# Second layer's output projection: three pairs of token tiles by seven block products instead of eight, with the sums that this takes on VectorE

## The chip, the cores and the metric

The kernel runs on one NeuronCore of one Trainium2 chip. The metric is the device time of one execution in microseconds (us): 958.06 us is the median of three runs of the kernel before (957.97, 958.06 and 960.04 us).

## The reference

Two layers of a decoder trunk work on 1,024 tokens of width 1,024. In each layer an input projection feeds three groups of heads (windowed attention, retention, gated linear attention); their outputs are gated, joined to a mix of width 1,024 and projected back:

```
y = jnp.concatenate([a_out, r_out, g_out], axis=-1) @ w_out
return x + gate * rms_norm(y, post_gain)
```

The change concerns this product `mix @ w_out` of the second layer, which is the last large work of the program. Everything is f32 in and out.

## The kernel before

**Two halves for one number.** TensorE works on f32r operands. To keep f32 accuracy each operand is held as a high part (`hi`, the value rounded to f32r) and a low part (`lo`, the rest), and a product takes three passes: hi by hi, lo by hi, hi by lo (`PASSES`). Each operand therefore costs one rounding copy (ScalarE or VectorE) and one subtraction (VectorE or GpSimd) before TensorE can use it.

**The output projection** (`y_half`, L1278 to L1286) takes one tile of 128 tokens and one half of 512 output columns at a time: 8 steps over the width by 3 passes are 24 matmuls of 128x512 into one of three PSUM banks called `mm`. The token tile is the stationary operand, the weights are the moving one; the two 256-column units of a half are read as one operand of two segments (`both`). There are 8 token tiles by 2 halves. ScalarE squares the result for the norm (L1285, with a sum over the row), VectorE multiplies it by the gain (L1286). The last half of the last tile is split into two of 256 columns (`y_last`, L1288 to L1305), so that the sums of the norm are nearly done when the last matmul ends.

**The finish** of a tile (`finish`, L1325 to L1334) loads the tile's residual from `xs` in HBM (SyncE's queue), forms `yg * r + x` on VectorE (L1330), and stores it from ScalarE's queue (`sx`), which stands in order with ScalarE's arithmetic: a store that waits for VectorE holds what ScalarE has to do behind it.

**The mix** reaches the projection through HBM. `head_norm_gate` (L1007) and `gate` (L1508) round the gated head outputs, subtract, and store both halves to `mixS`; `load_mix` (L1307) reads 1 MB per tile. The `gate` results of tokens 512 to 1,023 come late: while the projection of the first tiles runs, TensorE still has some attention products to make between its matmuls.

**What sets the order.** TensorE's instructions keep the order in which the code emits them (with generators, `job` and `pump`, that let other work in between products at due times from the table `L`). On the other engines a scheduler orders the instructions; each engine and each queue then works strictly in that order.

**Memory.** The weights and the transposed tokens share two arenas of places 0 to 6 (`PLACES`, `TOK`); small work buffers come from pools: `t2` (14 of 128x512), `st` (5), `smx` (6), `mx` (2 of 1 MB).

## Time and profile before

| | us |
|---|---|
| median of three runs | 958.06 |
| the profiled execution | 954.65 |
| its span, first to last instruction | 952.9 |
| TensorE busy in the span | 932.7 |
| VectorE busy | 637.4 |
| ScalarE busy | 474.1 |
| GpSimd busy | 222.6 |

The profiled execution was one of the shorter ones: it lies 3.4 us under the median of the runs. A profile row gives start, duration, engine, line, operation, tiles out and in, and in brackets how long the engine had been idle and what ended that. `PE` is TensorE, `DVE` VectorE, `ACT` ScalarE, `POOL` GpSimd, `SPq` and `ACTq` the queues that issue transfers.

### The profile page before, as it was taken

The page shows a single profiled execution, that of the slowest core. Times are in us where ns is not written, and L with a number is a line of the kernel's source. Part 1 is how long each engine was busy: PE and PEld are TensorE (multiplying, and loading weights), DVE is VectorE, ACT ScalarE, POOL GpSimd, SP SyncE. Part 2 cuts the span into 40 slices and gives each one's busy share as a digit, 9 for nine tenths or more (in the row PEclk, how much of TensorE's full clock was granted, in tenths as well). Part 3 has the DMA queues.
Part 4 walks back from the last instruction along what each step waited for, and adds up shares of the span by engine and source line. Part 5 has one row for each costly group of instructions (what it writes and reads, how often), then busy time and mean ns, then how long its engine had stood idle before and what let it go on. Part 6 is the DMA issues. An engine that isn't in the chain of part 4 may idle for free.

```text
span 952.9 us, 15951 instructions
## 1 busy us (share of the span) xinstructions
PE 932.7 (98%) x5645; PEld 770.1 (81%) x5645; DVE 637.4 (67%) x1372; ACT 474.1 (50%) x1157; POOL 222.6 (23%) x288
## 2 busy tenths in 40 slices
...
GB/s 320 323 135 122 161 84 122 196 49 115 107 200 80 100 133 189 226 253 256 171 169 175 92 187 32 101 187 67 56 101 111 94 82 81 166 177 177 308 200 66
DMA packets 124651, 142.26 MB, mean 149 GB/s; under 512 B 11566, under 2 KB 95384, under 8 KB 124572
## 3 DMA queue, kind: packets, MB, share of 16 engines
...
## 4 chain that ended last, share of the span: by engine, by line
PE 85%; DVE 3%; issue 2%; ACT 2%; POOL 0%; DMA 0%; DVEq 0%; SPq 0%; POOLq 0%; ACTq 0%
PE mm L171 67%; PE aux L171 14%; PE aux L186 4%; ACT smx L971 0%; DMA t<-tabS 0%; ACT L1026 0%; DVE t L856 0%; ACT L1025 0%; DVE t L1029 0%; DVE t L1027 0%; DVE t L157 0%; ACT mx L1160 0%; DVE smx L966 0%; DVE arena L508 0%; DVE arena L149 0%
## 5 line engine op out<-in xcount | busy, mean ns | idle before, releaser
L171 PE MATMUL mm<-arena,arena 128*128 128x512 f32 (+2 forms) x1512 | 309.6, 358 | 0.0
L171 PE MATMUL mm<-arena 128*128 128x512 f32 (+2 forms) x1392 | 285.8, 359 | 0.0
L171 PEld LDWEIGHTS mm<-arena,arena 128*128 128x128 f32 x1512 | 246.5, 189 | 40.1 <-issue 2.1
L171 PEld LDWEIGHTS mm<-arena 128*128 128x128 f32 x1392 | 228.9, 190 | 37.2 <-issue 1.2
L171 PE MATMUL mm<-arena,mx 128*128 128x512 f32 (+1 forms) x696 | 157.3, 384 | 0.0
L171 PEld LDWEIGHTS mm<-arena,mx 128*128 128x128 f32 x696 | 126.5, 188 | 26.1 <-issue 1.5
L508 POOL TENSOR_TENSOR arena<-st,arena 128x512 fp32r<-128x512 f32 x57 | 85.9, 1512 | 158.0 <-ACT arena L147 100.3
L147 ACT ACTIVATE t<-aux 128x512 f32<-128x512 f32 x64 | 37.1, 591 | 82.6 <-PE aux L186 39.6
L508 DVE TENSOR_TENSOR arena<-st,arena 128x512 fp32r<-128x512 f32 x63 | 63.0, 1014 | 6.9 <-ACT arena L147 3.5
L147 ACT ACTIVATE arena<-st 128x512 fp32r<-128x512 f32 x82 | 48.4, 623 | 31.1 <-PE mm L171 15.0
L1285 ACT ACTIVATE t<-mm 128x512 f32<-128x512 f32 x30 | 17.9, 598 | 91.0 <-PE mm L171 46.3
L971 ACT ACTIVATE smx<-smx,sm 128x129 f32<-128x129 f32 x128 | 50.1, 394 | 18.1 <-DVE sm L968 17.9
L975 POOL TENSOR_TENSOR smx<-smx,sm 128x512 f32<-128x512 f32 x32 | 35.2, 1099 | 82.5 <-DVE sm L974 78.7
L384 DVE SCALAR_TENSOR_TENSOR acc<-st,c_act,acc 128x512 f32<-128x512 f32 x60 | 45.6, 760 | 13.1 <-DMA st<-in_w_mod_dram 12.1
L562 POOL TENSOR_TENSOR sm<-sm,few 128x1 f32<-128x1 f32 x26 | 14.8, 570 | 150.3 <-DVE sm L561 147.6
L1286 DVE TENSOR_TENSOR t<-mm,modg 128x512 f32<-128x512 f32 x30 | 20.7, 689 | 42.4 <-ACT t L1285 42.4
L1330 DVE SCALAR_TENSOR_TENSOR t<-t,sm,t 128x512 f32<-128x512 f32 x32 | 25.5, 827 | 30.8 <-DMA t<-xs 15.7
L186 PE MATMUL aux<-c_ident,t 128*128 128x128 f32 x224 | 33.7, 274 | 4.1 <-DVE t L634 2.3
L186 PEld LDWEIGHTS aux<-c_ident,t 128*128 128x128 f32 x224 | 26.6, 140 | 10.5 <-DVE t L634 2.7
L966 DVE COPY_PREDICATED smx<-c_curmask,aux 128x256 f32<-128x256 int32 x64 | 25.5, 447 | 12.8 <-ACT smx L147 11.4
L370 POOL MEMSET acc<- 128x512 f32 x4 | 2.1, 529 | 130.2 <-PE aux L171 119.1
L851 DVE TENSOR_TENSOR t<-mm,sincos 128x128 f32<-128x128 f32 (+2 forms) x36 | 16.2, 450 | 23.7 <-ACT t L147 12.5
...
## 6 DMA issues: line engine op xcount, KB each, us to landing
...
```

The source lines that it names most:

```text
L147: A.activation(dst, src, AF.Copy)
L171: T.matmul(dst, lhsT, rhs, start=start, stop=stop)
L186: T.transpose(dst, src, idn)
L384: V.scalar_tensor_tensor(acc, wt, c_act[:, k:k + 1], acc, ALU.mult, ALU.add)
L508: i = (G if first == 0 and kc in LOG else V if first == 0 else eng(f"wlo{kc}")).tensor_tensor(wt[:, 1, 2 * kc:2 * kc + 2, 0:256], st, f(hi ...
L851: V.tensor_tensor(a4, s4, cs.unsqueeze(1).unsqueeze(1).to_broadcast((P, nh, 2, 32)), ALU.mult)
L966: V.copy_predicated(sv, curmask.unsqueeze(1).to_broadcast((P, 2, P)), pv[:, :, n // P - 1, :])
L971: A.activation(sm[:, h, :], sm[:, h, :], AF.Exp, bias=mx[:, h:h + 1], accum_out=sums[:, h:h + 1])
L975: eng("pn").tensor_tensor(sm[:, :, 0:128], sm[:, :, 0:128], rs.unsqueeze(2).to_broadcast((P, 4, P)), ALU.mult)
L1285: A.activation(yg, pm, AF.Square, accum_out=ss[:, nh:nh + 1])
L1286: V.tensor_tensor(yg, pm, modg[l][:, 512 * nh:512 * nh + 512], ALU.mult)
L1330: V.scalar_tensor_tensor(xt[j], yg[j], r, xt[j], ALU.mult, ALU.add)
```

## The change

In the second layer, token tiles 0 and 1 are still projected with 24 matmuls per half (`y_std`), halves 1 of both tiles first. Tiles 2 to 7 go in three pairs (`y_pair`). For a pair the tokens (2 tiles), the width (2 halves of 512) and the columns (2 halves of 512) make a 2x2 by 2x2 block product. Instead of eight block products (12 matmuls each: 4 steps by 3 passes) it makes seven, with sums of the operands and of the results (Winograd's form of Strassen's scheme).

- Four sums of weight blocks are made once, in four chunks of 128 rows (`combine`): the four blocks of a chunk are fetched from HBM again as f32, VectorE makes four differences, ScalarE and VectorE make `hi` and `lo` of the results. They go into places 0, 1, 2 and, after tiles 0 and 1 have used it for their half 1, place 4 (`combine_last`).
- Four sums of token blocks are made for each pair (`operands`): seven `hi`/`lo` pairs in all. For this the mix of tiles 2 to 7 is stored and loaded as plain f32 (`mixF`), and `gate` and `head_norm_gate` no longer split it.
- The results: `c11` is the sum of two products, `c21`, `c22` and `c12` take running sums. Bank `a` accumulates products 1, 6, 5 and 3 on top of each other, and ScalarE copies it out after products 1, 6 and 5 (L1423, L1431, L1438); the next product may add to the bank only when that copy is done. Bank `c` holds product 7 (copied out, L1434) and then product 4 on top.
- `y_last` is gone, in the first layer too; for tile 7 one half of the residual sum moves to ScalarE (scaling) and GpSimd (sum), and its store to SyncE's queue (`late`).

The engine of every sum is set in the table `EN` (`ct0` to `ct3`, `co1` to `co7`, `cs1` to `cs4`, `cg`, `cg2`: all VectorE). The diff, cut to its core:

```diff
+    mixF = dr.tile([NT, P, KT, P], F32, name="mixF")
...
-        copy("mh", sh, g1)
-        V.tensor_tensor(sl, g1, f(sh), ALU.subtract)
-        for a, (k, m) in enumerate((("smh", sh), ("sml", sl))):
-            dma(k, mixS[2 * p:2 * p + 2, :, a, kt0:kt0 + 2, :].rearrange("t p k q -> p t k q"),
-                f(m).rearrange("p (t k q) -> p t k q", t=2, k=2))
+        if l == DEPTH - 1 and p:
+            dma("smh", mixF[2 * p:2 * p + 2, :, kt0:kt0 + 2, :].rearrange("t p k q -> p t k q"),
+                g1.rearrange("p (t k q) -> p t k q", t=2, k=2))
+        else:
+            copy("mh", sh, g1)
+            V.tensor_tensor(sl, g1, f(sh), ALU.subtract)
+            for a, (k, m) in enumerate((("smh", sh), ("sml", sl))):
+                dma(k, mixS[2 * p:2 * p + 2, :, a, kt0:kt0 + 2, :].rearrange("t p k q -> p t k q"),
+                    f(m).rearrange("p (t k q) -> p t k q", t=2, k=2))
...
-    def y_last(l, mixt, ss, yg):
...
+    def load_block(l, kh, nh):
+        b = blk(BLK[kh][nh])
+        for i in range(4):
+            st = stage()
+            dma("lw", st, w_rows(l, 4 * kh + i, nh))
+            hi, lo = b[:, 0, i, :], b[:, 1, i, :]
...
+                copy(f"whi{i}", hi, st)
+                eng(f"wlo{i}").tensor_tensor(lo, st, f(hi), ALU.subtract)
+
+    def wide():
+        return gp.tile([P, 4, 129], F32, tag="smx", name=nm("wide"), bufs=SMB).rearrange("p h n -> p (h n)")[:, 0:512]
+
+    def fetch_chunk(l, i):
+        tl = []
+        for kh, nh in ((0, 0), (0, 1), (1, 1), (1, 0)):
+            t_ = wide() if i % 2 else stage()
+            dma("lw", t_, w_rows(l, 4 * kh + i, nh))
+            tl.append(t_)
+        return tl
...
+    def put(k, hi, lo, src):
+        A.activation(hi, src, AF.Copy)
+        eng(k).tensor_tensor(lo, src, f(hi), ALU.subtract)
+
...
+        V.tensor_tensor(b11, b12, b11, ALU.subtract)
+        less(b12, b22, b12)
+        less(b22, b22, b11)
+        less(b21, b21, b22)
+        for n, t_ in ((1, b22), (0, b11), (2, b12)):
+            put(f"ct{n}", blk(n)[:, 0, i, :], blk(n)[:, 1, i, :], t_)
+        return b21
+
+    def combine_last(i, t_):
+        b = blk(BLK[0][1])
+        put("ct3", b[:, 0, i, :], b[:, 1, i, :], t_)
...
+            for kh in range(2):
+                a = t2() if p == 1 or len(res) == 1 else stage()
+                dma("lmix", a.rearrange("p (k q) -> p k q", k=4), mixF[t, :, 4 * kh:4 * kh + 4, :])
+                res.append(a)
+        return res
...
+    def operands(raw):
+        a11, a12, a21, a22 = raw
...
+        for n, src, tag in (("1", a11, "kT0"), ("2", a12, "kT1")):
+            o = gp.tile([P, 1024], F32R, tag=tag, name=nm("op"), bufs=1)
+            keep(n, o[:, 0:512], o[:, 512:1024], src)
+        s1, s2 = wide(), wide()
+        eng("cs1").tensor_tensor(s1, a21, a22, ALU.add)
+        eng("cs2").tensor_tensor(s2, s1, a11, ALU.subtract)
+        eng("cs3").tensor_tensor(a21, a11, a21, ALU.subtract)
+        yield res
+        x = mix_tile().rearrange("p a k q -> p (a k q)")
+        keep("6", x[:, 0:512], x[:, 512:1024], s2)
+        keep("7", x[:, 1024:1536], x[:, 1536:2048], a21)
+        eng("cs4").tensor_tensor(a12, a12, s2, ALU.subtract)
+        x = mix_tile().rearrange("p a k q -> p (a k q)")
+        keep("5", x[:, 0:512], x[:, 512:1024], s1)
+        keep("4", x[:, 1024:1536], x[:, 1536:2048], a22)
+        hi, lo = [gp.tile([P, 512], F32R, tag="st", name=nm("op"), bufs=BST) for _ in range(2)]
+        keep("3", hi, lo, a12)
+        yield res
+
+    def product(dst, a, b, start):
...
+        for x, y in PASSES:
+            for k in range(4):
+                mult(dst, a[x][:, k, :], b[:, y, k, :], start and q == 0, q == 11, None, not start)
...
+    def y_pair(l, p, o, soon):
+        t0, t1_ = 2 * p, 2 * p + 1
+        last = p == NP_ - 1
+        a, b, c = mm(), mm(), mm()
+        g0, g1 = modg[l][:, 0:512], modg[l][:, 512:1024]
+        sA, sB = small(2), small(2)
+        product(a, o["1"], blk(BLK[0][0]), True)
+        c11 = wide()
+        A.activation(c11, a, AF.Copy)
+        product(b, o["2"], blk(BLK[1][0]), True)
+        V.tensor_tensor(c11, b, c11, ALU.add)
+        A.activation(b, c11, AF.Square, accum_out=sA[:, 0:1])
+        eng("cg").tensor_tensor(c11, c11, g0, ALU.mult)
+        soon(0)
+        product(a, o["6"], blk(1), False)
+        c21 = wide()
+        A.activation(c21, a, AF.Copy)
+        product(c, o["7"], blk(2), True)
+        m7 = t2()
+        A.activation(m7, c, AF.Copy)
+        soon(1)
+        product(a, o["5"], blk(0), False)
+        c22 = t2()
+        i0 = A.activation(c22, a, AF.Copy)
+        i1 = V.tensor_tensor(c22, c22, m7, ALU.add)
+        A.activation(m7, c22, AF.Square, accum_out=sB[:, 1:2])
+        eng("cg2").tensor_tensor(c22, c22, g1, ALU.mult)
+        with tc.issue_after(i0.ins), tc.issue_after(i1.ins):
+            soon(2)
+        product(c, o["4"], blk(BLK[0][1]), False)
+        V.tensor_tensor(c21, c, c21, ALU.add)
+        A.activation(c, c21, AF.Square, accum_out=sB[:, 0:1])
+        V.tensor_tensor(c21, c21, g0, ALU.mult)
+        job(finish(l, t1_, sB, [c21, c22], None, (0,) if last else ()))
+        pump()
+        soon(3)
+        c12 = t2()
+        b22 = blk(BLK[1][1])
+        if not last:
+            product(a, o["3"], b22, False)
+            A.activation(c12, a, AF.Square, accum_out=sA[:, 1:2])
+            V.tensor_tensor(c12, a, g1, ALU.mult)
+            job(finish(l, t0, sA, [c11, c12]))
+            pump()
+            return
...
+        V.tensor_scalar(r, sA[:, 0:1], 1.0 / D, EPS, ALU.mult, ALU.add)
+        product(a, o["3"], b22, False)
+        sq = A.activation(c12, a, AF.Square, accum_out=sA[:, 1:2])
+        q = V.scalar_tensor_tensor(r, sA[:, 1:2], 1.0 / D, r, ALU.mult, ALU.add)
+        root = G.tensor_tensor(r, r, mhalf[:, 0:1], ALU.pow)
+        with tc.issue_after(sq.ins), tc.issue_after(root.ins):
+            for x, y, r7, t, sl in late:
+                A.activation(y, y, AF.Copy, scale=r7)
+                G.tensor_tensor(x, y, x, ALU.add)
+        for x, y, r7, t, sl in late:
+            dma("lx", out[0, t * P:(t + 1) * P, sl], x)
         with tc.issue_after(q.ins):
-            V.tensor_tensor(yg[:, c], pm, modg[l][:, 768:1024], ALU.mult)
-        return r
+            V.tensor_tensor(c12, a, g1, ALU.mult)
+        job(finish(l, t0, sA, [c11, c12], r))
+        pump()
+
+    def last_output(l):
+        mx = [load_mix(l, t) for t in range(2)]
...
+        chunk = {0: fetch_chunk(l, 0), 1: fetch_chunk(l, 1)}
+        raw = load_pair(l, 1)
...
+        for n, (nh, t) in enumerate(((1, 0), (1, 1), (0, 0), (0, 1))):
+            y_std(l, t, nh, mx[t], ss[t], yg[t][nh])
+            held[n] = combine(l, n, chunk.pop(n))
+            if n < 2:
+                chunk[n + 2] = fetch_chunk(l, n + 2)
+            if n == 1:
+                for i in range(2):
+                    combine_last(i, held.pop(i))
+            if nh == 0:
+                job(finish(l, t, ss[t], yg[t]))
+                pump()
+            if n == 2:
+                prep = operands(raw)
+                o = next(prep)
+        for i in (2, 3):
+            combine_last(i, held.pop(i))
+        next(prep)
...
+        for p in range(1, NP_):
+            def soon(i, p=p):
+                if p + 1 < NP_:
+                    if i == 0:
+                        nxt["raw"] = load_pair(l, p + 1)
+                    elif i == 2:
+                        nxt["prep"] = operands(nxt["raw"])
+                        nxt["o"] = next(nxt["prep"])
+            y_pair(l, p, o, soon)
+            if p + 1 < NP_:
+                next(nxt["prep"])
+                o = nxt["o"]
...
+    late = []
...
+            if j in side:
+                late.append((xt[j], yg[j], r, t, sl))
+                continue
+            else:
+                V.scalar_tensor_tensor(xt[j], yg[j], r, xt[j], ALU.mult, ALU.add)
...
+            whole = (4, 2 if hf == 0 else 0)[l == DEPTH - 1]
+            if whole < 4:
+                dma("sm0", mixF[4 * hf + whole:4 * hf + 4, :, k, :].rearrange("t p q -> p t q"),
+                    ao[:, whole * P:].rearrange("p (t q) -> p t q", q=P))
+            if whole:
+                w_ = slice(0, whole * P)
+                mh, ml = t2(F32R), t2(F32R)
+                copy("mg", mh[:, w_], ao[:, w_])
+                eng("mgl").tensor_tensor(ml[:, w_], ao[:, w_], f(mh[:, w_]), ALU.subtract)
+                for a, m in ((0, mh), (1, ml)):
+                    dma(f"sm{a}", mixS[4 * hf:4 * hf + whole, :, a, k, :].rearrange("t p q -> p t q"),
+                        f(m[:, w_]).rearrange("p (t q) -> p t q", q=P))
...
+        if l == DEPTH - 1:
+            last_output(l)
+            return
...
-MIXP = (6, 7)
+BLK = ((3, 4), (5, 6))
```

TensorE, the last half of tile 1 and the products of tiles 2 and 3, before (each `mm` is a fresh use of one of the three PSUM banks, `mx` the tokens' halves, `arena` the weights):

```order
L171 MATMUL mm_9478<-arena_357,mx_9312 128x512 x24
L171 MATMUL mm_9524<-arena_357,mx_9429 128x512 x24
L171 MATMUL mm_9565<-arena_357,mx_9429 128x512 x24
L171 MATMUL mm_9611<-arena_357,mx_9518 128x512 x24
L171 MATMUL mm_9638<-arena_357,mx_9518 128x512 x24
```

TensorE, tiles 2 and 3 now (`op` and `mx` hold the operands' halves, `mm_9578` is bank a, `mm_9579` b, `mm_9580` c):

```order
L171 MATMUL mm_9578<-arena_358,op_9498 128x512 x12
L171 MATMUL mm_9579<-arena_358,op_9501 128x512 x12
L171 MATMUL mm_9578<-arena_73,mx_9563 128x512 x12
L171 MATMUL mm_9580<-arena_73,mx_9563 128x512 x12
L171 MATMUL mm_9578<-arena_73,mx_9569 128x512 x12
L171 MATMUL mm_9580<-arena_358,mx_9569 128x512 x12
L171 MATMUL mm_9578<-arena_358,op_9574 128x512 x4
L171 MATMUL mm_9578<-arena_358,op_9575 128x512 x4
L171 MATMUL mm_9578<-arena_358,op_9574 128x512 x4
```

Before, tiles 2 and 3 are the last four rows, 96 matmuls, and each row goes to a bank of its own; now they are 84 matmuls, and bank a takes four of the seven products, each on top of what stands there (its last one is the last three rows, bank c takes two).

ScalarE, where tiles 1 to 3 are squared and stored, before (`mm_9435` and `mm_9478` are tile 1, `mm_9524` and `mm_9565` tile 2; L160 are the stores of a finished tile):

```order
L1285 ACTIVATE t_1666_9433,sm_9432<-mm_9435 128x512
L1285 ACTIVATE t_1667_9434,sm_9432<-mm_9478 128x512
L160 DMA out_dram<-t_1676_9510 128x512
L160 DMA out_dram<-t_1677_9511 128x512
L1285 ACTIVATE t_1680_9522,sm_9521<-mm_9524 128x512
L1285 ACTIVATE t_1681_9523,sm_9521<-mm_9565 128x512
L160 DMA out_dram<-t_1690_9597 128x512
L160 DMA out_dram<-t_1691_9598 128x512
```

ScalarE now, from the stores of tile 0 (`t_1685`, `t_1686`) to the third copy out of bank a:

```order
L160 DMA out_dram<-t_1685_9490 128x512
L160 DMA out_dram<-t_1686_9491 128x512
L1412 ACTIVATE t_1658_9302,sm_9299<-mm_9509 128x512
L1326 ACTIVATE mx_9569<-wide_9504 128x512
L1326 ACTIVATE mx_9569<-t_1653_9296 128x512
L1423 ACTIVATE wide_9595<-mm_9578 128x512
L160 DMA out_dram<-t_1694_9551 128x512
L160 DMA out_dram<-t_1695_9552 128x512
L1426 ACTIVATE mm_9579,sm_9581<-wide_9595 128x512
L1431 ACTIVATE wide_9636<-mm_9578 128x512
L1434 ACTIVATE t_1711_9650<-mm_9580 128x512
L1438 ACTIVATE t_1712_9664<-mm_9578 128x512
```

Before, only squares stood behind the stores of a tile; now the copies L1423 and L1431, which bank a's next product needs, stand behind the stores of tiles 0 and 1.

VectorE, the finish of tile 1 and the work on tile 2, before (L1330 is the residual sum):

```order
L1330 SCALAR_TENSOR_TENSOR t_1676_9510<-t_1666_9433,sm_9507,t_1676_9510 128x512
L1330 SCALAR_TENSOR_TENSOR t_1677_9511<-t_1667_9434,sm_9507,t_1677_9511 128x512
L1286 TENSOR_TENSOR t_1680_9522<-mm_9524,modg_6071 128x512
L1286 TENSOR_TENSOR t_1681_9523<-mm_9565,modg_6071 128x512
L567 TENSOR_TENSOR sm_9592<-sm_9521 128x1
L561 TENSOR_SCALAR sm_9594<-sm_9592 128x1
```

VectorE now, from the residual sums of tile 0 (L1540) to the first sum of results (L1425); L1728 are two gates of the attention, L1327 makes the low part of an operand, L1413 multiplies tile 1's last half by the gain:

```order
L1540 SCALAR_TENSOR_TENSOR t_1685_9490<-t_1656_9300,sm_9487,t_1685_9490 128x512
L1540 SCALAR_TENSOR_TENSOR t_1686_9491<-t_1657_9301,sm_9487,t_1686_9491 128x512
L1728 SCALAR_TENSOR_TENSOR t_1681_9466<-t_1629_9215,t_1681_9466 128x512
L1728 SCALAR_TENSOR_TENSOR t_1682_9468<-t_1639_9265,t_1682_9468 128x512
L1413 TENSOR_TENSOR t_1658_9302<-mm_9509,modg_6044 128x512
L568 TENSOR_TENSOR sm_9546<-sm_9299 128x1
L1327 TENSOR_TENSOR mx_9569<-wide_9504,mx_9569 128x512
L562 TENSOR_SCALAR sm_9548<-sm_9546 128x1
L1327 TENSOR_TENSOR mx_9569<-t_1653_9296,mx_9569 128x512
L1540 SCALAR_TENSOR_TENSOR t_1694_9551<-t_1658_9302,sm_9548,t_1694_9551 128x512
L1540 SCALAR_TENSOR_TENSOR t_1695_9552<-t_1659_9303,sm_9548,t_1695_9552 128x512
L1425 TENSOR_TENSOR wide_9595<-mm_9579,wide_9595 128x512
```

Before, the residual sums were followed by gain products that had only their squares to wait for; now two gates, low parts of operands and tile 1's residual sums stand in one row ahead of the first sum of results.

106 lines of the change are left out of this document (67 added, 39 removed).

## The prediction

> **What bounds the kernel now.** I read the page first, then the windows, the chain and the timeline of the end. All times are places in the profiled execution.
>
> ```profile
> span 952.9 us, 15951 instructions
> PE 932.7 (98%) x5645; PEld 770.1 (81%) x5645; DVE 637.4 (67%) x1372; ACT 474.1 (50%) x1157; POOL 222.6 (23%) x288
> ...
> PE 85%; DVE 3%; issue 2%; ACT 2%; POOL 0%; DMA 0%; DVEq 0%; SPq 0%; POOLq 0%; ACTq 0%
> ```
>
> The busy share of PE alone says little; the chain does: 85% of it is PE. So the windows of the second output projection (granted clock in the third column from the right), and the chain's piece there:
>
> ```profile
> core 0: us, PE busy (x) PEld busy (x) DVE busy (x) ACT busy (x) POOL busy (x), PEclk, DMA share, GB/s
> ...
> 871.00:924.00 53.00, 53.00 (x237) 43.73 (x234) 17.66 (x33) 6.80 (x19) 2.31 (x4) 1.00 0.83 276
> 924.00:947.00 23.00, 23.00 (x125) 19.89 (x123) 6.50 (x15) 3.23 (x10) 1.10 (x2) 1.00 0.12 46
> 947.00:953.00 6.00, 0.06 (x1) 0.00 (x0) 1.91 (x4) 0.47 (x2) 0.55 (x1) 0.75 0.23 87
> ```
>
> ```profile
> 871.27 70.05 PE mm L171 x308
> ```
>
> The projection is one unbroken run of matmuls, 70.05 us for 308, which is 0.2274 us each, at full clock. VectorE works 17.66 of 53 us beside it and ScalarE 6.80. A matmul less there is time saved, as long as the other two keep up.
>
> **What it removes.** Before, 7 tiles and a half make 15 x 24 = 360 matmuls of 128x512; the last half makes 48 of 256 columns. Their price comes from the squares that follow them, here with the rest of the tail (ACT squares, DVE and POOL make the root, DVE the residual sum, ACTq stores):
>
> ```profile
> 944.28 0.39 ACT L1295 ACTIVATE t<-mm 128x256 f32<-128x256 f32 x1 [2.25 <-PE mm L171]
> ...
> 947.10 0.38 ACT L1295 ACTIVATE t<-mm 128x256 f32<-128x256 f32 x1 [2.34 <-DMA out_dram<-t]
> 947.38 0.19 ACT L1295 ACTIVATION_READ_ACCUMULATOR t<-mm 128x1 f32 x1
> 947.60 0.16 DVE L1301 SCALAR_TENSOR_TENSOR sm<-sm 128x1 f32<-128x1 f32 x1 [2.05 <-ACT t L1295]
> 947.68 0.42 DVE L1304 TENSOR_TENSOR t<-mm,modg 128x256 f32<-128x256 f32 x1
> 947.84 0.55 POOL L1302 TENSOR_TENSOR sm<-sm,few 128x1 f32<-128x1 f32 x1 [4.20 <-DVE sm L1301]
> 948.43 1.41 DVE L1330 SCALAR_TENSOR_TENSOR t<-t,sm,t 128x512 f32<-128x512 f32 x2 [0.33 <-POOL sm L1302]
> 949.21 1.00 ACTq L160 DMA_DIRECT2D out_dram<-t  x2
> ```
>
> 24 of them took 947.10 - 944.28 = 2.82 us, 0.1175 each. Now there are 4 x 24 + 3 x 84 = 348, all 128x512. PE loses 360 x 0.2274 + 48 x 0.1175 - 348 x 0.2274 = 2.73 + 5.64 = 8.37 us. The moving operand is now one run of 512 columns, not two of 256; two 256-column matmuls cost 0.2350, more than the 0.2274 of one split one, so I take the same price. If the split itself costs something, at most about the 0.0076 between these two, 348 matmuls gain up to 2.6 us; no row shows an unsplit 512, so that stays an outer end, and I take none of it. The work taken from `gate` and `head_norm_gate`, and `y_last` of the first layer (0.18 us), lie beside a PE that is busy, or are too small to count.
>
> **What it adds on VectorE.** Sums and low parts: 32 rows for the weights, 33 for three sets of operands, 9 more on the results. What one costs:
>
> ```profile
> 707.28 0.69 DVE L1020 TENSOR_TENSOR t<-t,t 128x512 fp32r<-128x512 f32 x1 [0.92 <-ACT t L147]
> 707.89 0.68 DVE L1144 TENSOR_TENSOR t<-t,t 128x512 f32<-128x512 f32 x1
> 708.50 0.68 DVE L1145 TENSOR_TENSOR t<-t,t 128x512 f32<-128x512 f32 x1
> ...
> 739.79 0.69 DVE L1027 TENSOR_TENSOR t<-t,t 128x512 f32<-128x512 f32 x1 [3.11 <-issue]
> 740.52 0.69 DVE L1029 TENSOR_TENSOR t<-aux,t 128x512 f32<-128x512 f32 x1
> ```
>
> Independent ones start 0.61 apart, dependent ones 0.73; the residual sums above take 1.41 for two, 0.71 each. A later pair has 20 large rows, some 14 us, in 84 x 0.2274 = 19.1 us of PE: VectorE keeps up there. Pair 1 is the tight one, since the weights' sums stand in front of it. When must they be there? These rows give the ends of the first four halves before, which keep their place, and when VectorE was free of the gates ahead of them:
>
> ```profile
> 854.66 1.04 POOL L975 TENSOR_TENSOR smx<-smx,sm 128x512 f32<-128x512 f32 x1 [1.30 <-DVE sm L974]
> ...
> 854.76 1.48 DVE L1518 SCALAR_TENSOR_TENSOR t<-t,t 128x512 f32<-128x512 f32 x1 [0.25 <-DMA t<-aoS]
> ...
> 881.57 0.60 ACT L1285 ACTIVATE t<-mm 128x512 f32<-128x512 f32 x1 [4.81 <-PE mm L171]
> ```
>
> The fourth half ends by about 881.4. Pair 1's products take 12 x 0.2274 = 2.73 us: product 6, the first with summed weights, is due at 881.4 + 5.46 = 886.9, product 5 at 892.3.
>
> VectorE is free at 854.76 + 1.48 = 856.2. From there to the last low part before tile 0's residual sums (in the order of VectorE) stand 33 sums, 7 with a scalar and 3 small ones: 33 x 0.61 + 7 x 0.71 + 3 x 0.17 = 25.6 us, so 881.8 at best. Some depend on the row before; the 1.48 above, 0.8 over the usual 0.69 with GpSimd at work, shows what the last attention pieces on GpSimd add. I allow 3.2 us: 885.0. The operands of products 6 and 7 are ready before that. Up to here PE waits for nothing.
>
> **The wait it adds.** Now tile 0's two residual sums (to 886.5), two gates (887.9), a gain product and two low parts with small ones (890.0), then tile 1's residual sums. Those need a load from `xs`, which stands in SyncE's queue behind the store of the first gate (887.2, two issues of 0.4). How long such a load takes, and what its store does to ScalarE, the rows of the kernel before show:
>
> ```profile
> 898.63 1.41 DVE L1330 SCALAR_TENSOR_TENSOR t<-t,sm,t 128x512 f32<-128x512 f32 x2 [4.57 <-DMA t<-xs]
> 899.41 1.05 ACTq L160 DMA_DIRECT2D out_dram<-t  x2
> 900.56 0.60 ACT L1285 ACTIVATE t<-mm 128x512 f32<-128x512 f32 x1 [7.49 <-DMA mx<-mixS]
> ...
> 903.27 0.60 ACT L1285 ACTIVATE t<-mm 128x512 f32<-128x512 f32 x1 [2.02 <-PE mm L171]
> ...
> 905.08 15.10 SPq L160 DMA_DIRECT2D t<-xs  x8
> ...
> 910.37 1.42 DVE L1330 SCALAR_TENSOR_TENSOR t<-t,sm,t 128x512 f32<-128x512 f32 x2 [5.43 <-DMA t<-xs]
> ```
>
> Issued at 905.08, used at 910.37: 5.3 us. And the square at 900.56 was due one half (24 x 0.2274 = 5.46) before the one at 903.27, at 897.8: it stood 2.7 us behind two stores that waited for the residual sums. That cost PE nothing, with three banks for fresh products. Now behind these stores stand the copies out of bank a, and PE may not add to the bank before they are done.
>
> - Copy 1 (L1423): residual sums of tile 0 end 886.5, one issue 0.35, then ScalarE's square 0.8, two high parts and the copy 0.6 each: 889.5. Product 6 waits 2.6 us.
> - Copy 2 (L1431): tile 1's load is used at 887.6 + 5.3 = 892.9, its sums end at 894.4, the first sum of results at 895.1; square 0.8, copy 0.6, hand-overs 0.2: 896.7. Product 5, due at 892.3, waits until then: 4.4 us in all, the first 2.6 among them.
>
> I take 4.5. The ends: at 3 us per load and no allowance on VectorE the wait is 0 to 1; with 7 us per load, or 4 us more on VectorE, it is 8. Pairs 2 and 3 have their residuals loaded early and no gates between; I take nothing for them.
>
> **The tail.** Before, the last square and its sum took 0.57 us, the product under the root 0.42; now 0.8 and 0.69, which is 0.3 more in the chain. GpSimd's sum for tile 7 (1.04 by the row at 854.66) runs beside the last residual sums; the 1.48 at 854.76 was such an overlap. I take 0.3 for it, 0.6 together; bounds 0.2 and 1.4.
> The Trainium skill, "GPSIMD Engine Reference", section 1 Specifications, says that GpSimd shares its SBUF interfaces with VectorE and contends with its instructions of two SBUF inputs: by that rule each microsecond of GpSimd costs VectorE about one, and the tail 1.3 us; the 1.48 beside 1.04 bears it out. The sum keeps 0.6, as the sums' own overlap is short.
>
> **The sum.** -8.4 + 4.5 + 0.6 = -3.3 us: 951.35 for the profiled execution's 954.65, and against the median of 958.06, 954.8 us. A measurement of this kernel can tell about 0.2% (1.9 us) from no change.
>
> **The rivals.**
>
> - *Nothing stands in PE's way.* The loads come in 3 us and VectorE runs at 0.61. Then a wait of 0.5 is left: -8.4 + 0.5 + 0.6, 950.8 us. For it: VectorE had 35 of 53 us free. Against: everything added lands in the first 35 of these. Chance 0.13.
> - *VectorE becomes the bound.* Each of some 50 rows from 856 to product 5 needs its ScalarE half first and sits beside late attention; at 0.85 us each, midway between 0.69 and the 1.0 that such rows reach beside GpSimd, they end 50 x 0.2 = 10 us later, the wait is 14.5, and the time 958.06 - 8.4 + 14.5 + 0.6 = 964.8. It turns slower from a wait of 7.8 us on, so 3.3 us later than forecast. A row for the price:
>
> ```profile
> L1521 DVE TENSOR_TENSOR t<-t,t x16: 679/693/1003, 357.7 to 884.7; 128x512 fp32r<-128x512 f32 x16
> ```
>
>   The median, 0.693, speaks against it. Chance 0.17.
> - *The clock falls in the wait.* The 6 us at the end, with PE idle, have a granted clock of 0.75. If two to four products after the waits run at that, each costs 2.73 x (1/0.75 - 1) = 0.9 more: 1.8 to 3.6, 956.6 to 958.4. Against it: waits of 2.6 and 1.8 us with a product or two between. Chance 0.08.
>   The Trainium skill, "TensorE: Matmul & The Clock Gate", Part 1, has the clock halved after an idle window of about 3.4 us; by that rule neither wait alone is enough, one of 4.5 us would be. The 0.75 agrees with a clock that falls when idle.
> - *The weights' second fetch comes late.* 4 MB more are read while the DMA engines are up to 0.83 busy (871 to 924); but the mix of six tiles shrinks from 6 to 3 MB. If a chunk comes 8 us late, the slack of 886.9 - 883 is spent and 4 us are added: 958.8. Chance 0.07.
>
> The forecast (wait 2.5 to 6.5 us, 952.8 to 956.8) has 0.55. For 8 in 10 the range runs from 950.3 to 960.0: it takes in most of the no-wait case, the clock, the late fetch, and the near end of the VectorE case. Faster by over 0.2%: the no-wait case and most of the forecast, 0.59; within 0.2%: the forecast's end, the clock, a late fetch, 0.22; slower: 0.19, mostly VectorE.
>
> **What would show it.** PE: 84 matmuls in 19.1 us for pairs 2 and 3, without gaps. Gaps of 2 to 3 us ahead of product 6 and of 1 to 3 ahead of product 5 of pair 1, ended by ScalarE's copies L1423 and L1431; ahead of these, ScalarE idle for stores that wait for L1540, and VectorE idle there for `t<-xs`. It is wrong if PE waits for L1327 (low parts) or for the weights' chunks, if gaps recur in pairs 2 and 3, if 12 matmuls do not take 2.73 us, or if the tail after the last matmul is over 1.4 us longer.

## The result, and the profile after

The changed kernel takes 953.19 us (median of four runs, 952.75 to 954.33), the kernel before beside it 958.16 (957.97 to 960.04). The ratio is 0.9946, with a 95% interval of 0.9928 to 0.9963: 5.0 us less, where 3.3 less were forecast.

The two profiled executions differ by less. After, the execution took 952.75 us (span 951.0); before, 954.65. Where the missing 3 us are is taken up with the last experiment. The page of the changed kernel:

```profile
span 951.0 us, 15893 instructions
PE 925.5 (97%) x5561; PEld 760.3 (80%) x5561; DVE 673.2 (71%) x1425; ACT 497.8 (52%) x1197; POOL 228.6 (24%) x291
...
PE 85%; DMA 5%; DVE 4%; issue 3%; ACT 2%; POOL 1%; SPq 0%; DVEq 0%; ACTq 0%; POOLq 0%
```

PE is busy 7 us less, VectorE 36 us more; the chain is still 85% PE. The windows of the second output projection, in the same columns as before (span of the window, busy time of each engine, granted clock third from the right):

```profile
871.00:884.00 13.00, 13.00 (x63) 10.27 (x60) 13.00 (x24) 7.00 (x14) 0.00 (x0) 1.00 0.36 116
884.00:900.00 16.00, 13.11 (x50) 10.34 (x50) 8.63 (x16) 4.03 (x10) 1.86 (x2) 0.89 0.81 265
```

VectorE has no free moment from 871 to 884; PE is idle for 2.89 of the 16 us after that, at a mean clock of 0.89. The timeline of pair 1 shows the idle time from both sides:

```profile
884.55 0.67 DVE L1327 TENSOR_TENSOR op<-t,op 128x512 fp32r<-128x512 f32 x1
...
885.67 1.42 DVE L1540 SCALAR_TENSOR_TENSOR t<-t,sm,t 128x512 f32<-128x512 f32 x2 [0.45 <-POOL sm L563]
886.46 1.02 ACTq L160 DMA_DIRECT2D out_dram<-t  x2
...
887.60 0.60 ACT L1412 ACTIVATE t<-mm 128x512 f32<-128x512 f32 x1 [3.91 <-DVE t L1540]
...
888.14 1.08 SPq L160 DMA_DIRECT2D t<-xs  x2
...
889.23 0.59 ACT L1423 ACTIVATE wide<-mm 128x512 f32<-128x512 f32 x1
...
889.86 12.80 PE L171 MATMUL mm<-arena,mx 128*128 128x512 f32 x48 [2.89 <-ACT wide L1423]
...
891.88 1.48 DVE L1540 SCALAR_TENSOR_TENSOR t<-t,sm,t 128x512 f32<-128x512 f32 x2 [1.53 <-DMA t<-xs]
...
893.27 0.68 DVE L1425 TENSOR_TENSOR wide<-mm,wide 128x512 f32<-128x512 f32 x1
...
894.62 0.58 ACT L1431 ACTIVATE wide<-mm 128x512 f32<-128x512 f32 x1
...
899.99 0.60 ACT L1438 ACTIVATE t<-mm 128x512 f32<-128x512 f32 x1 [2.12 <-PE mm L171]
...
919.03 0.60 ACT L1438 ACTIVATE t<-mm 128x512 f32<-128x512 f32 x1 [2.12 <-PE mm L171]
...
938.07 0.60 ACT L1438 ACTIVATE t<-mm 128x512 f32<-128x512 f32 x1 [2.12 <-PE mm L171]
```

Read it from PE's row back: product 6 starts at 889.86 after 2.89 us of waiting for copy 1 (L1423). That copy comes behind a square (L1412), and ahead of that square ScalarE had been idle for 3.91 us: there stand the stores of tile 0, which wait for its residual sums (L1540). The three last rows give a pair's length: 899.99, 919.03, 938.07, so 19.04 us for 84 matmuls, 0.2267 each. From copy 3 of pair 1 on there is no room for a gap.

The row of PE holds something else: 48 matmuls in 12.80 us, where 48 x 0.2267 is 10.9. Copy 2 (L1431) ended at 895.2, before product 5 could start, so there was no second wait. What was slow shows in finer windows of the same kernel:

```profile
890.00:892.00 2.00, 2.00 (x7) 1.63 (x8) 0.47 (x2) 0.00 (x0) 0.76 (x1) 0.75 0.92 272
892.00:894.00 2.00, 2.00 (x6) 1.54 (x5) 1.96 (x3) 0.01 (x1) 0.00 (x0) 0.50 0.86 311
894.00:896.00 2.00, 2.00 (x9) 1.60 (x9) 0.69 (x1) 1.20 (x3) 0.00 (x0) 0.90 0.82 207
```

The clock falls to 0.5 about 1 us after PE has started again, and is back at 1.00 before 895: half of 890 to 892, all of 892 to 894 and a fifth of 894 to 896 make 3.4 us at 0.5.

Last, the tail of the changed kernel in the timeline:

```profile
943.50 0.60 ACT L1463 ACTIVATE t<-mm 128x512 f32<-128x512 f32 x1 [1.22 <-PE mm L171]
943.99 0.75 DVE L1540 SCALAR_TENSOR_TENSOR t<-t,sm,t 128x512 f32<-128x512 f32 x1 [0.67 <-POOL sm L563]
944.00 0.20 ACT L1463 ACTIVATION_READ_ACCUMULATOR t<-mm 128x1 f32 x1
944.66 0.15 DVE L1464 SCALAR_TENSOR_TENSOR sm<-sm,sm 128x1 f32<-128x1 f32 x1
...
945.54 0.75 DVE L1540 SCALAR_TENSOR_TENSOR t<-wide,sm,t 128x512 f32<-128x512 f32 x1
945.96 1.48 POOL L1469 TENSOR_TENSOR t<-wide,t 128x512 f32<-128x512 f32 x1 [0.45 <-ACT wide L1468]
946.21 1.78 DVE L1540 SCALAR_TENSOR_TENSOR t<-t,sm,t 128x512 f32<-128x512 f32 x1
```

From the start of the last square to the end of the span it is 951.0 - 943.5 = 7.5 us; before it was 952.9 - 947.1 = 5.8. Of the 1.7 more, 0.2 is the longer square. The square is done at 944.20, but L1464, which takes its sum, starts at 944.66, behind tile 7's own residual sum: 0.46. And the last residual sum takes 1.78 us beside GpSimd's sum of 1.48 where the one ahead of it takes 0.75: 1.03.

So the trace of the change shows two things that the sum did not have: a clock that falls after a wait of under 3 us, and a tail three times as dear as the 0.6 us taken for it. The experiments take them one by one.

### The profile page after: what moved, and what is told of

The parts are those of the page before. It is cut to its first block, busy times and chain, and to the rows that moved or that the text cites. A ratio compares the mean times of both kernels' runs of the same rounds, so it can differ in the third digit from the quotient of the medians.

```text
span 951.0 us, 15893 instructions
## 1 busy us (share of the span) xinstructions
PE 925.5 (97%) x5561; PEld 760.3 (80%) x5561; DVE 673.2 (71%) x1425; ACT 497.8 (52%) x1197; POOL 228.6 (24%) x291
## 4 chain that ended last, share of the span: by engine, by line
PE 85%; DMA 5%; DVE 4%; issue 3%; ACT 2%; POOL 1%; SPq 0%; DVEq 0%; ACTq 0%; POOLq 0%
PE mm L171 67%; PE aux L171 14%; PE aux L186 4%; DMA xk<-in_x_dram 1%; DMA aoS<-t 1%; DMA t<-mixF 1%; DMA wm<-in_w_mod_dram 1%; DMA st<-in_w_in_dram 0%; DMA wide<-in_w_out_dram 0%; DVE arena L1327 0%; DMA t<-in_x_dram 0%; ACT smx L972 0%; DMA t<-aoS 0%; DMA t<-tabS 0%; ACT L1027 0%
## 5 line engine op out<-in xcount | busy, mean ns | idle before, releaser
L171 PE MATMUL mm<-arena,arena 128*128 128x512 f32 (+2 forms) x1392 | 287.6, 359 | 0.0
L171 PEld LDWEIGHTS mm<-arena,arena 128*128 128x128 f32 x1392 | 227.2, 189 | 37.5 <-issue 2.1
L171 PE MATMUL mm<-arena,mx 128*128 128x512 f32 x624 | 148.4, 395 | 2.9 <-ACT wide L1423 2.9
L171 PEld LDWEIGHTS mm<-arena,mx 128*128 128x128 f32 x624 | 117.0, 190 | 28.8 <-ACT wide L1423 3.3
L509 POOL TENSOR_TENSOR arena<-st,arena 128x512 fp32r<-128x512 f32 x53 | 79.7, 1510 | 155.5 <-ACT arena L147 97.6
L509 DVE TENSOR_TENSOR arena<-st,arena 128x512 fp32r<-128x512 f32 x55 | 54.0, 996 | 6.7 <-ACT arena L147 3.6
L563 POOL TENSOR_TENSOR sm<-sm,few 128x1 f32<-128x1 f32 x27 | 16.8, 622 | 145.8 <-DVE sm L562 132.1
L655 ACT ACTIVATE t<-aux,mod,mod 128x128 f32<-128x128 f32 x56 | 21.2, 455 | 20.3 <-PE aux L186 12.1
L1028 DVE TENSOR_TENSOR t<-t,t 128x512 f32<-128x512 f32 x16 | 11.1, 691 | 29.3 <-ACT t L1027 26.2
L1540 DVE SCALAR_TENSOR_TENSOR t<-t,sm,t 128x512 f32<-128x512 f32 x26 | 21.1, 827 | 14.5 <-DMA t<-in_x_dram 9.6
```

The source lines that it names most:

```text
L171: T.matmul(dst, lhsT, rhs, start=start, stop=stop, skip_group_check=more)
L509: i = (G if first == 0 and kc in LOG else V if first == 0 else eng(f"wlo{kc}")).tensor_tensor(wt[:, 1, 2 * kc:2 * kc + 2, 0:256], st, f(hi ...
L563: after[2] = G.tensor_tensor(r, r, mhalf[:, :w], ALU.pow)
L655: A.activation(hf[:, ks], pt[:, ks], AF.Identity, scale=gain, bias=shift)
L1540: V.scalar_tensor_tensor(xt[j], yg[j], r, xt[j], ALU.mult, ALU.add)
```

## The experiments

Two theories stood at their start. Theory A is the forecast's: the copies out of bank a come late because ScalarE stands at the stores of tiles 0 and 1, and the fall of the clock and the tail come on top. The rival is that VectorE is the bound at this place, full as it is from 871 to 884, and that the wait would only move.

The part of an execution ahead of the projection scatters, by 2 us over the ten profiles of the changed kernel and its variants and by 4 us over the four of the kernel before. So beside the medians I give the time from one mark to the end: the mark is the start of the 32 matmuls of 7.49 us near 762 us, which both kernels have, ahead of everything that the change does to the projection. For the changed kernel it is 952.75 - 761.47 = 191.28 us.

**The wait's place: the finish of tiles 0 and 1 later.**

```
  for n, (nh, t) in enumerate(((1, 0), (1, 1), (0, 0), (0, 1))):
...
-     if nh == 0:
-         job(finish(l, t, ss[t], yg[t]))
-         pump()
...
      y_pair(l, p, o, soon)
+     if p == 1:
+         for t in range(2):
+             job(finish(l, t, ss[t], yg[t]))
+             pump()
```

> The end of tiles 0 and 1 (their reciprocal norm, the loads of the residual, the four residual sums of L1540 and the four stores) is emitted behind pair 1's products in place of behind each tile's own; nothing else moves. Theory A (the copies of pair 1 out of bank a stand on ScalarE behind the stores of tiles 0 and 1, which wait for VectorE's residual sums): copy 1 ends right behind product 1, TensorE waits for under 0.3 us ahead of product 6 and not at all ahead of product 5, the clock stays at 1.00, and the time is 4.0 to 4.8 us less than that of the changed kernel. Rival B (VectorE's late low parts hold the pair up, whatever ScalarE does): the low part of operand 6 or the sum of L1425 still ends last ahead of product 6 or product 7, the wait stays at 2 us or more, and the time is within 1 us of the changed kernel.

Measured: 949.15 us (947.71 to 949.83), ratio to before 0.9904 (0.9892 to 0.9917), 4.0 under the changed kernel. From the mark on it is 186.24 us. Its timeline:

```profile
885.59 0.58 ACT L1423 ACTIVATE wide<-mm 128x512 f32<-128x512 f32 x1
...
887.83 11.04 PE L171 MATMUL mm<-arena,mx 128*128 128x512 f32 x48
```

Copy 1 ends 1.7 us before product 6, the row of product 6 has no idle time in it, and 48 matmuls take 11.04 us. VectorE was as full as before (13.00 of 13 us from 871 to 884), so its low parts were not the bound. This is theory A, with the size that it asked for. But the edit takes the residual sums out of VectorE's row as well as the stores out of ScalarE's; which of the two held PE, it does not say.

**The stores alone.**

```
- dma("sx", out[0, t * P:(t + 1) * P, sl] if l == DEPTH - 1 else xs[t, :, sl], xt[j])
+ dma("lx" if l == DEPTH - 1 and t < 2 else "sx", out[0, t * P:(t + 1) * P, sl] if l == DEPTH - 1 else xs[t, :, sl], xt[j])
```

> The four stores of tiles 0 and 1 go out on SyncE's queue in place of ScalarE's; nothing else differs from the changed kernel. Theory A (it is these stores, standing on ScalarE and waiting for the residual sums, that hold copy 1): copy 1 ends before 887, and product 6 waits for under 0.3 us. Copy 2 still stands behind the square of the sum L1425, which VectorE does only after tile 1's residual sums (893.3 in the changed kernel), so it ends at about 896 and product 5, due at 892.4, waits 3 to 4 us: the wait moves on rather than going, and the time is 0 to 1.5 us under that of the changed kernel. Rival B (copy 1 is held by something else on ScalarE or by VectorE): the wait ahead of product 6 stays at 2 us or more.

Measured: 952.51 us (951.38 to 953.96), ratio 0.9941 (0.9925 to 0.9958); 189.37 from the mark on. Its timeline:

```profile
885.17 0.59 ACT L1423 ACTIVATE wide<-mm 128x512 f32<-128x512 f32 x1
...
892.94 0.68 DVE L1425 TENSOR_TENSOR wide<-mm,wide 128x512 f32<-128x512 f32 x1
...
894.28 0.58 ACT L1431 ACTIVATE wide<-mm 128x512 f32<-128x512 f32 x1
...
894.91 5.74 PE L171 MATMUL mm<-arena,mx 128*128 128x512 f32 x24 [2.03 <-ACT wide L1431]
```

The copy that held product 6 now ends at 885.8, with the residual sums still in their place, so the stores were what held it. The wait moves on to product 5, as expected, but is 2.03 us, not 3 to 4: copy 2 ended at 894.9. Both halves of the forecast's chain are in these rows, the stores ahead of copy 1, and L1425 behind tile 1's residual sums ahead of copy 2. To take one away brings little while the other stands. (From the start of the last square to the end this execution took 8.2 us in place of 7.5, which hides 0.7 of what it gained.)

**Another order of products in pair 1.**

```
- product(a, o["6"], blk(1), False)
- c21 = wide()
- A.activation(c21, a, AF.Copy)
  product(c, o["7"], blk(2), True)
  m7 = t2()
  A.activation(m7, c, AF.Copy)
+ product(a, o["6"], blk(1), False)
+ c21 = wide()
+ A.activation(c21, a, AF.Copy)
...
- product(a, o["5"], blk(0), False)
...
  product(c, o["4"], blk(BLK[0][1]), False)
...
+ product(a, o["5"], blk(0), False)
```

> Pair 1 alone takes its products in the order 1, 2, 7, 6, 4, 5, 3 in place of 1, 2, 6, 7, 5, 4, 3; all sums stay. Product 7 needs no copy, so copy 1 out of bank a has one product more of time (2.7 us), and product 4 stands between 6 and 5; product 3 follows 5 on bank a directly. Theory A (TensorE waits only because the copies out of bank a come late): the wait of 2.89 us ahead of product 6 falls to about 0.2, the clock stays at 1.00 there and saves 1.8, product 3 then waits for copy 2 for about 0.8: 3.7 to 4.0 us less than the changed kernel. Rival B (VectorE is the bound at this place: it is full from 871 to 885 us, and the wait would only move on to the next product): the idle time of TensorE between 884 and 900 us stays at 2 us or more, and the time is within 1 us of the changed kernel.

Measured: 952.51 us (951.39 to 954.23), ratio 0.9942 (0.993 to 0.9953); 189.87 from the mark on. The time is the rival's, within 1 us of the changed kernel; of the 3.7 to 4.0 us that theory A expected nothing came. From its timeline:

```profile
888.43 0.69 DVE L1413 TENSOR_TENSOR t<-mm,modg 128x512 f32<-128x512 f32 x1
...
889.18 5.74 PE L171 MATMUL mm<-arena,mx 128*128 128x512 f32 x24 [1.25 <-DVE t L1413]
...
895.61 5.76 PE L171 MATMUL mm<-arena,mx 128*128 128x512 f32 x24 [0.69 <-ACT t L1454]
...
902.05 2.33 PE L171 MATMUL mm<-arena,op 128*128 128x512 f32 x9 [0.69 <-ACT t L1465]
```

2.6 us in three waits, 1.94 of them between 884 and 900, where the rival asked for 2 or more. In its single steps theory A was half right: product 6 did not wait at all, the clock stayed at 1.00, and product 3 waited 0.69 us for copy 2 (L1465 in this kernel), forecast 0.8. What it left out are the other two waits. I had said that product 7 needs no copy. It needs its bank, and bank c is the one from which VectorE takes tile 1's last half (L1413), behind tile 0's residual sums and two gates: 1.25 us. Product 4 then waits 0.69 for the copy of product 7 (L1454), on ScalarE behind the square of the sum L1425, which VectorE makes only after tile 1's residual sums. So at this place VectorE's row stands in the way as well, though not its low parts: the residual sums, of which e3_later clears both engines.

**The clock: filling the idle time.**

```
+ if p == 1:
+     spare = aux()
+     for q_ in range(12):
+         mult(spare, o["1"][0][:, q_ % 4, :], blk(BLK[0][0])[:, 0, q_ % 4, :], q_ == 0, q_ == 11)
  product(a, o["6"], blk(1), False)
```

> Twelve more matmuls of 128x512 (operand 1's high part by block W11's high part, into an accumulator bank of their own that nobody reads) stand between products 2 and 6 of pair 1, so that TensorE has 12 x 0.227 = 2.7 us of work in the place where the changed kernel leaves it idle for 2.89 us. Everything else is computed as in the changed kernel. Theory A (the idle time itself costs 2.9 us, and the clock that falls to 0.5 after it costs another 1.8 us): the idle time is only filled, so it stays paid for, but the granted clock stays at 1.00 from 884 to 900 us and products 6 and 7 take 5.5 us, not 7.3: 1.8 us less than the changed kernel, about 951.4 where that has 953.2. If copy 2 then ends too late for product 5, up to 1.8 of it comes back as a wait there. Rival B (the records' clock is only a figure, products 6 and 7 are slow for another reason, such as the copies and VectorE's work on the same banks): 7.3 us again, and no difference in time.

Measured: 952.32 us (951.71 to 953.43), ratio 0.994 (0.9928 to 0.9951). The window behind the wait, and the row of product 6 in the timeline:

```profile
891.00:897.00 6.00, 6.00 (x26) 4.83 (x27) 3.28 (x5) 1.44 (x4) 0.89 (x1) 1.00 0.81 261
```

```profile
891.00 11.30 PE L171 MATMUL mm<-arena,mx 128*128 128x512 f32 x48 [0.23 <-ACT wide L1423]
```

The clock stays at 1.00 and the 48 matmuls take 11.30 us in place of 12.80: the 1.5 us were the clock's, not the copies'. The median does not resolve it: it lies 0.9 us under the changed kernel's, where 1.8 were expected, with intervals that overlap. VectorE was 1.1 us later in this execution (its loads of `mixF` landed later), and product 2 waited 0.80 us for a bank out of which VectorE still had to take a result (L1413), so from the mark on only 0.5 of the 1.5 shows (190.80); from the start of product 6 to the end it is 952.32 - 891.00 = 61.32 us, against 952.75 - 889.86 = 62.89.

**How long an idle time it takes: four filler matmuls, and the changed kernel once more.** The edit against e1_filler:

```
- for q_ in range(12):
-     mult(spare, o["1"][0][:, q_ % 4, :], blk(BLK[0][0])[:, 0, q_ % 4, :], q_ == 0, q_ == 11)
+ for q_ in range(4):
+     mult(spare, o["1"][0][:, q_ % 4, :], blk(BLK[0][0])[:, 0, q_ % 4, :], q_ == 0, q_ == 3)
```

> As e1_filler, with 4 filler matmuls in place of 12 (operand 1's high part by block W11's, into a bank that nobody reads; all else is computed as in the changed kernel): TensorE's idle time ahead of product 6 is cut from 2.89 to about 2.0 us. Theory A (the clock falls only after an idle time longer than some bound between the 1.25 us of e2_order, where it stayed at 1.00, and 2.89): if the bound is over 2.0, the granted clock stays at 1.00 from 890 to 896 us, products 6 and 7 take 5.5 us and the time is about 1.5 us under that of the changed kernel; if it is under 2.0, the clock falls to 0.5 there as in the changed kernel and the time is the same. Rival B (the clock falls by the share of idle time in a longer stretch): it falls in part, to a mean of 0.8 to 0.95 from 890 to 896, and 0.3 to 1.0 us are lost.

> The changed kernel, unchanged, once more, on the same chip as e8_fill4. Theory A (its wait and its clock are the same in every execution): product 6 waits 2.6 to 3.2 us for copy 1, the clock falls to 0.5 within 2 us after it, the time from the last square's start to the end is 7.5 us, and the median is 952.5 to 954. Rival B (the fall of the clock after so short an idle time is an accident of one execution): the clock stays at 1.00 from 890 to 896 in this profile, and the median lies under 952.5.

Measured: 953.27 us (950.68 to 956.3) with four fillers, 953.45 (952.27 to 954.81) for the changed kernel, ratios 0.995 (0.9934 to 0.9966) and 0.995 (0.9933 to 0.9968). With four fillers, PE waited 1.97 us and the clock stayed (timeline, windows):

```profile
887.49 3.03 PE L171 MATMUL mm<-arena,op 128*128 128x512 f32 x12 [1.11 <-DVE t L1413]
...
893.40 11.20 PE L171 MATMUL mm<-arena,mx 128*128 128x512 f32 x48 [1.97 <-ACT wide L1423]
```

```profile
894.00:896.00 2.00, 2.00 (x10) 1.67 (x9) 0.75 (x1) 0.00 (x0) 0.29 (x1) 1.00 0.97 274
```

That the time is nevertheless the same has two reasons. One is the first row: VectorE was 1.4 us later here than in the changed kernel (again the loads of `mixF`), and product 2 waited 1.11 us for L1413, so that from the mark on this execution took 190.99 us. The other is on the other side of the comparison: the changed kernel itself, in its second profile (timeline, windows), had no fall to lose:

```profile
891.74 11.50 PE L171 MATMUL mm<-arena,mx 128*128 128x512 f32 x48 [2.80 <-ACT wide L1423]
```

```profile
894.00:896.00 2.00, 2.00 (x11) 1.64 (x9) 1.90 (x3) 0.00 (x0) 0.00 (x0) 1.00 0.72 246
```

So the wait is always there (2.80 and 2.89), the fall of the clock is not: rival B was right on the clock, theory A on the wait, the tail and the median. The third profile with this wait is that of the next experiment, e4_tail, whose timeline shows a wait of 2.90 us, and whose clock fell as in the first:

```profile
891.12 12.79 PE L171 MATMUL mm<-arena,mx 128*128 128x512 f32 x48 [2.90 <-ACT wide L1423]
```

Idle times of 2.89 and 2.90 brought it, 2.80, 2.03, 1.97 and 1.25 did not. By length alone that would be a bound between 2.80 and 2.89. But the traces also hold the moments at which the clock changes, and in each of the fourteen profiles these lie whole steps of 3.413 us apart (in the changed kernel 24.00, 890.99 and 894.40: 254 steps and one). So here are windows that are laid along these steps. In the changed kernel:

```profile
887.58:890.99 3.41, 1.13 (x5) 0.95 (x6) 2.73 (x7) 2.21 (x5) 0.93 (x1) 1.00 0.94 286
890.99:894.40 3.41, 3.41 (x10) 2.67 (x9) 2.08 (x3) 0.41 (x1) 0.00 (x0) 0.50 0.85 302
```

In e4_tail:

```profile
888.89:892.30 3.41, 1.18 (x5) 1.01 (x6) 2.67 (x7) 2.17 (x5) 0.93 (x1) 1.00 0.91 295
```

In the second profile of the changed kernel:

```profile
889.96:893.37 3.41, 1.63 (x7) 1.35 (x8) 2.23 (x6) 1.73 (x5) 0.93 (x1) 1.00 0.90 281
```

PE was idle for 2.28 and 2.23 us of the one step that ended with the fall. In the third execution the wait of 2.80 us lay across two steps, 1.02 us in one and 1.78 in the next, and the clock stayed; of the waits in e5_store, e8_fill4 and e2_order no step held more than 1.68. The ends of the executions narrow it: behind a step with 1.87 us of idle time the clock stayed (e8_fill4, 943.86 to 947.27), behind one with 2.13 it fell (the changed kernel, 942.19 to 945.60). Here, then, the moment decides: what counts is how much of the idle time falls into one step, and the bound lies between 1.87 and 2.13 us. That holds for this projection only. Near the start of the program, among other matmuls, the clock of the kernel before fell at 35.25 us after a step in which PE had not been idle.

Where the clock stays, the 48 matmuls take 11.50 us against 11.04 without any wait (e3_later). Of the second wait that I forecast, 0.5 us is therefore the most that can be there: the weights of product 5 did wait 0.40 us for copy 2. From the mark on this execution took 953.27 - 763.49 = 189.78 us, 1.50 less than the one whose clock fell.

**The tail: no sum on GpSimd.**

```
- job(finish(l, t1_, sB, [c21, c22], None, (0,) if last else ()))
+ job(finish(l, t1_, sB, [c21, c22], None, ()))
```

> In the last pair, tile 7's first residual sum goes to VectorE (L1540) like all the others, in place of ScalarE's scaling and GpSimd's sum (L1468, L1469) at the very end. Theory A (GpSimd's sum of 1.48 us slows the last residual sum on VectorE, which takes 1.78 us beside it and 0.75 us without): each sum takes about 0.75 us, the stretch from TensorE's last matmul to the end shrinks from 7.5 to 6.2 to 6.8 us, and the time is 0.7 to 1.3 us less than that of the changed kernel. Rival B (the tail is set by the number of sums that VectorE has to do one after the other): one sum of 0.7 us more on VectorE, and the time is the same or up to 0.7 us more.

Measured: 953.58 us (952.29 to 954.72), ratio 0.9953 (0.9941 to 0.9965). The same time as the changed kernel. The tail in its timeline:

```profile
944.75 0.60 ACT L1463 ACTIVATE t<-mm 128x512 f32<-128x512 f32 x1 [1.22 <-PE mm L171]
945.24 0.75 DVE L1540 SCALAR_TENSOR_TENSOR t<-wide,sm,t 128x512 f32<-128x512 f32 x1 [0.67 <-POOL sm L563]
...
945.91 0.75 DVE L1540 SCALAR_TENSOR_TENSOR t<-t,sm,t 128x512 f32<-128x512 f32 x1
...
946.57 0.15 DVE L1464 SCALAR_TENSOR_TENSOR sm<-sm,sm 128x1 f32<-128x1 f32 x1
...
948.12 0.75 DVE L1540 SCALAR_TENSOR_TENSOR t<-t,sm,t 128x512 f32<-128x512 f32 x1
```

Each theory has half of it, and the halves work against each other. The last sum takes 0.75 us without GpSimd beside it (1.03 less), but L1464 now starts 1.8 us behind the square's start in place of 1.2, behind two sums. From the last square's start to the end it is 951.8 - 944.75 = 7.05 us in place of 7.5: 0.4 in the trace, too little for the medians.

**Both edits, and an earlier root for tile 7.** The second kernel adds this to the first (in the last pair; the others keep their order):

```
+ if last:
+     r7 = small(1)
+     V.tensor_tensor(r7, sB[:, 0:1], sB[:, 1:2], ALU.add)
+     i7 = V.tensor_scalar(r7, r7, 1.0 / D, EPS, ALU.mult, ALU.add)
+     G.tensor_tensor(r7, r7, mhalf[:, 0:1], ALU.pow)
+     with tc.issue_after(i7.ins):
+         V.tensor_tensor(c21, c21, g0, ALU.mult)
...
- V.tensor_tensor(c21, c21, g0, ALU.mult)
- job(finish(l, t1_, sB, [c21, c22], None, ()))
+ job(finish(l, t1_, sB, [c21, c22], r7, ()))
```

> The two edits e3_later and e4_tail together: the end of tiles 0 and 1 behind pair 1's products, and all of tile 7's residual sums on VectorE. Theory A (the parts are independent): the 4.0 us of the first and the 0.4 us that the second takes off the tail in its trace, so 4.4 less than the changed kernel, 948.7. Rival B (the tail's two effects, a faster last sum and one more sum on VectorE, cancel): 949.2, the time of e3_later.

> As e6_both, and in the last pair the sum of squares for tile 7's root comes ahead of the product with the gate (L1447 in the changed kernel) on VectorE, so that GpSimd's root runs beside that product. Theory A (tile 7's residual sums stand in the way of the last square's sum on VectorE, by 0.46 us in the changed kernel and by 1.1 in e4_tail): they start 0.6 us earlier, and the time from the last square's start to the end falls from 7.05 us (e4_tail) to 6.4; the time is 0.6 less than that of e6_both, 948.1. Rival B (the last residual sums are bound by the last root, not by what stands ahead of it on VectorE): the tail stays at 7.0 and the time at that of e6_both.

Measured: 949.4 us (946.88 to 951.07), ratio 0.9903 (0.9888 to 0.9919), and 949.11 (948.1 to 949.64), ratio 0.9905 (0.989 to 0.992). Neither can be told from e3_later's 0.9904. Their last square starts at 940.86 and 939.72 and their spans end at 947.8 and 946.4: tails of 6.9 and 6.7 us, against 7.05 and 6.4 expected; the earlier root gave about half of what theory A asked of it. Against e3_later's own tail of 7.4 us (947.1 - 939.71) the traces give back 0.5 and 0.7 us, but the medians do not resolve it. The best kernel is e3_later or one of these, about 9 us under the kernel before.

**Where the other 1.6 to 3 us are: the kernel before, three times more.** The two profiles of the changed kernel are 1.9 and 3.4 us under the first one of before from the mark on; the medians differ by 5.0.

> The kernel before, unchanged, profiled once more. The two profiled executions differ by 1.9 us (954.65 and 952.75), the medians by 5.0 (958.16 and 953.19). Theory A (the first profiled execution of the kernel before was 3.5 us luckier than most of its executions, in a part that the change does not touch): this one takes 956.5 to 959.6 us; its extra time stands ahead of the second output projection, whose matmuls again take 0.227 us each in one unbroken run; and from the last square's start (ScalarE) to the end of the span it is 5.8 us again. Rival B (the extra time lies in the second output projection or the tail itself, so that the change saves more than its trace shows): the projection has gaps or a clock under 1.00 here, or its tail is over 7 us.

> The kernel before, unchanged, a third profile. From the start of the 32 matmuls of 7.49 us near 762 us on, both profiled executions of it took 193.17 us to the end of their time, and those of the changed kernel 191.28 (the clock fell) and 189.78 (it did not): 1.9 and 3.4 us less, where the medians differ by 5.0. Theory A (the rest, 1.6 to 3 us, lies ahead of that point, where most executions of the kernel before are slower than the two profiled): if this execution takes 957.5 to 959, the 32 matmuls start at 764.3 to 765.8, and 193.2 us follow again. Rival B (it lies behind that point): over 194 us follow.

> The kernel before, unchanged, a fourth profile; what each theory expects is as for e10_before.

Measured: 956.59, 958.11 and 958.86 us. The mark and the projection in the chain of the last of them, behind the group of 30 matmuls used below:

```profile
700.64 1.92 PE aux L171 x30
...
765.67 7.49 PE mm L171 x32
...
875.47 70.05 PE mm L171 x308
```

With the first profile, the marks of the four executions are 761.48, 763.42, 764.94 and 765.67; the time behind them is 193.17, 193.17, 193.17 and 193.19 us. In these four the projection and its tail do not vary, and all the scatter lies ahead of the mark. The ten profiles of the changed kernel and its variants have the mark at 761.47 to 763.68, mean 762.4; those of before have it at 763.9 in the mean. Theory A, then: the first profile of before, on which I made the sum, was early. But not all of it is scatter. From the start of a group of 30 matmuls near 700 us to the mark it is 62.83 and 62.79 us in the two profiles of the changed kernel and 62.78 to 62.82 in its eight variants, and 63.51, 64.18, 64.02 and 65.03 in those of before. Up to that group the means are equal (699.6 and 699.7 us). So the mean difference ahead of the mark, 1.4 us, lies in this stretch and goes with the change; with the 1.9 to 3.4 us behind the mark it makes 3.3 to 4.8 of the 5.0. PE's longest wait there, in the longest execution of before (us in total, times, longest):

```profile
PE aux L171 <- ACT t L1167: 1.1, 1, 1.1
```

and in the changed kernel:

```profile
PE aux L171 <- ACT t L1172: 0.2, 1, 0.2
```

L1167 and L1172 are the same copy on ScalarE. In the other profiles of before this wait is 0.2, 0.7 and 0.7 us, and all four have a wait of 0.4 us for VectorE (L868) that no profile of the changed kernel or its variants has. In that stretch the change takes splits and stores of the mix off ScalarE, VectorE and SyncE. That this is why the waits are shorter was not tried alone.

## Why the prediction was right, and where not

- **What PE loses: 8.37 us.** Right. 84 matmuls took 19.04 us in each pair, 0.2267 each against the 0.2274 assumed, 0.2 us more over 348. The gain of up to 2.6 for the unsplit operand is not there.
- **VectorE keeps up to product 6.** Right: the last low part was forecast to end at 885.0 and ended at 885.2, and PE never waited for a low part. A chunk of weights came late to VectorE (2.62 us of waiting ahead of 851.7), which cost PE nothing, so the late fetch did not come as a cost either. The rival "VectorE becomes the bound" did not come in the changed kernel: pairs 2 and 3 have no gap. But it was near. In e1_filler, e6_both and e8_fill4, where the loads of `mixF` landed 1.0 to 1.4 us later, product 2 waited 0.75 to 1.11 us for L1413 on VectorE, and in e2_order a wait of 1.25 us ended with the same line.
- **The wait ahead of product 6.** Right in cause and size: 2.89 and 2.80 us, forecast 2.6; copy 1 ended at 889.8, forecast 889.5. e3_later and e5_store show the cause.
- **The wait ahead of product 5.** The cause was right (e5_store has it at 2.03 us), the size not: at most 0.5 us where the clock stayed, none where it fell, forecast 1.8. The mis-sized term is the load from `xs`: 891.88 - 888.14 = 3.7 us from issue to use (4.1 in the second profile), not 5.3, so copy 2 ended at 895.2, not 896.7. The 5.3 was a misreading as well: the load that the sum at 910.37 waited for in the kernel before had been issued at 903.68, 6.7 us earlier, so that row, read rightly, would have put the term further off. Why the load was quicker in the changed kernel stays open.
- **The clock falls in the wait, 0.08.** Too low: it fell in two of three profiled executions that had this wait, after one wait of 2.89 and 2.90 us, and cost 1.3 to 1.6 us. I had held against it that the waits were short; what counted was how much of the wait lay in one step of 3.41 us, and 2.2 to 2.3 us were enough. The Trainium skill, "TensorE: Matmul & The Clock Gate", Part 1, has the clock fall after about one idle window of 3.4 us, in a window that runs freely. The steps of 3.41 us in these traces agree with the free window; that PE worked for 1.1 to 1.2 us of it does not agree with an idle one, and the measurement decides against taking 3.4 us as the least idle time.
- **The tail: 0.6, at most 1.4.** Wrong: 1.7, and over the bound that I had set. The longer square was there (0.2). The GpSimd sum cost 1.03, not 0.3. Not in the sum at all was tile 7's other residual sum on VectorE, 0.46 us in front of L1464. The Trainium skill, "GPSIMD Engine Reference", section 1 Specifications, has GpSimd and VectorE share their SBUF interfaces; the tail of 1.3 that I had worked out from that, and set aside because the overlap was short, was nearer than the 0.6 that I took: 1.78 us beside a GpSimd sum of 1.48, 0.75 without.
- **"Too small to count".** Wrong, as far as can be told: ahead of the mark, between about 700 and 762 us, the changed kernel is 0.7 to 2.2 us shorter, 1.4 in the mean. The work taken out of the gates of the second layer is the part of the change that reaches there; that it is the cause is argued, not shown.
- **The sum.** Against one execution of before: -8.4 + 4.5 + 0.6 = -3.3. From the mark on, the two profiles of the change give -3.39 (clock stays: 2.80 of wait and 0.46 more in the 48 matmuls behind it, tail 1.7) and -1.89 (clock falls: 2.89 + 1.76 lost in and behind the wait, tail 1.7). With the 8.6 that PE loses these add up to -3.6 and -2.2, so 0.2 to 0.4 us are in no term. That the first of them hits the forecast is luck, a sum of two errors: a wait 1.2 too long and a tail 1.1 too short. The rest of the 5.0 lies ahead of the mark: in the stretch from 700 us on, and in the first profile of before, which had come early.
